# A hybrid attention step on one core: paced stores of k and v, loads given out when source and buffer are ready, and a second buffer

## The chip, the core and the metric

The kernel runs on one core of a Trainium2 chip. The core's engines each work through an instruction queue of their own: PE (TensorE) multiplies matrices, DVE (VectorE), ACT (ScalarE) and POOL (GpSimd) do the elementwise work, and SP issues most of the transfers between memory (DRAM) and the core. Engines wait for one another by semaphores. The metric is the device time of one execution in microseconds (us), lower is better.

## What is computed

One layer of a decoder in float32, for a prompt of 512 tokens and for 8 samples of 4 new tokens each with 1024 past tokens in paged caches. Both groups share the weights.

```python
def prompt_layer(x, norm_in, w_in, b_gate, b_forget, cmp_pe, cmp_w, w_out):
    h = rmsnorm(x, norm_in)
    q_n, kv_n, gates, z_n, q_f, k_f, v_f, logf, z_f = project(h, w_in, b_gate, b_forget)   # h @ w_in
    kc, c_end = compress(kv_n[:, :, 0], cmp_pe[0], cmp_w[0])      # blocks of 32 rows -> one row
    vc, _ = compress(kv_n[:, :, 1], cmp_pe[1], cmp_w[1])
    ...                                                           # per 128 queries:
    o_n = nsa_block(...)   # compressed + selected blocks + sliding window, gated
    o_f = fox_block(...)   # causal attention with a forget term
    y = merge(x, o_n, z_n, o_f, z_f, w_out)                       # silu gates, @ w_out, residual
    return y, (kv_n[:, :, :4], jnp.stack([k_f, v_f], axis=2), logf, kv_n[:, T - w_keep:, 4:])
```

The sample layer does the same with `cache_nsa_kv[page_table]`, `cache_fox_kv[page_table]` and `state_nsa_win` ahead of the new rows. A final RMSNorm follows. The new k and v rows are outputs too, in token order.

## The kernel before

The 544 tokens (512 of the prompt, 32 of the samples) stand in the columns of `h_hi` and `h_lo`, a two-part split of the normalized input. The main loop `run_tiles` computes the input projection in 60 tiles of 128 output columns. A tile is made of four weight pieces; a piece `raw` (128x512) is loaded by SP, split by ACT into `whi` and by DVE into `wlo`, and used by 24 matmuls into `pz` (three products for each of 4 row blocks and 2 token halves). Five `raw` buffers are loaded ahead, and pieces are split two ahead of their use. After a tile, `pz` is scaled into `zt` (two buffers), and the tile's `post` stream treats it: for k and v tiles `store_natural` transposes `zt` on DVE into `nat` (two buffers) and SP writes it to the output (`out<-nat`), to the scratch `scr_n` where a later stage reads it back, and its sample rows to `scr_s`.

All other work is written as Python generators, the streams: `fox_sample` (cache pages `fpg` with two buffers: score pages gathered by POOL and transposed by DVE into `ft`, value pages multiplied by PE into `accv`), `compress` (rows `crow`, tables `cw`, the prompt's own rows `cz` read back from `scr_n`, transposed by DVE into `more`; results go through `vt` to `scr_kc`), `nsa_prompt` (which loads a table of distances `rel_c` from `scr_c`), `nsa_sample` (pages `spg`, transposed into `skt`), the mixing, and the output projection `w_out` at the end.

The order of every engine's queue is set when the program is built. A planner, `Clock`, keeps a modelled time for each engine, for SP's ring (`ring`) and for each buffer. Between two groups of matmuls `S.pump()` runs every stream that may go on: a stream that says `yield [tile]` is resumed when the planner has the tile ready, `yield "flag"` when the flag is set, `yield function` when the function holds. On the chip, each engine takes its queue in exactly that order and waits at an instruction whose operands are not ready, with everything behind it. A load that is given out right after the last reader of its buffer stands in SP's or POOL's queue until that reader is done.

A flag such as `nkv00`, `k0` or `v0` releases the streams that read a stored tile, and `post{t}` allows tile t+2 to take its `zt` buffer. In the kernel before both are set after all of a tile's stores are given out, twelve or so in one go.

Pages are loaded half by SP and half by POOL. All instructions are recorded by one helper, so that every row of the profile says L147; the names of the tiles tell the places apart.

Of the kernel before, what the change touches and what calls it, by code (L numbers as in the profile page):

```python
# [8 lines left out]
F32 = mybir.dt.float32  # L9
# [6 lines left out]
P = 128  # L16
# [4 lines left out]
SEQ = 512  # L21
# [162 lines left out]
class Streams:  # L184
# [58 lines left out]

    def take_nat(self, n=1):
        yield lambda: self.left["nat"] >= n
        self.left["nat"] -= n
# [28 lines left out]
def trunk_step(ctx, tc, x_prompt, x_sample, cache_nsa_kv, cache_fox_kv, cache_fox_logf, state_nsa_win,  # L275
# [27 lines left out]
    flags = S.flags  # L303
# [110 lines left out]
    tiles = []  # L414
    raws, wsp, last_w, loaded = {}, {}, {}, [0]
# [69 lines left out]
    def run_tiles(t0, t1):  # L485
        for t in range(t0, t1):
# [6 lines left out]
            zt = stg.tile([P, TOK], F32, name="zt", bufs=2)  # L493
            clock.parts[zt.tensor.name] = (TOK, HALF)
# [201 lines left out]
    def store_natural(zt, dst_p, dst_s, keep_at=None):  # L696


        yield from S.take_nat()
        nat = stg.tile([P, TOK // 32, 32], F32, name="nat", bufs=2)  # L700
        yield [nat]
        nc.vector.transpose(nat.rearrange("p t f -> p (t f)"), zt)
        yield [nat]
        by_token = lambda ap, at, row, q: dram(ap, at + q * 32, [[row, 32], [32 * row, SEQ // 32], [1, 32]])
        for q in range(4):
            rows = nat[q * 32:q * 32 + 32]
            nc.sync.dma_start(by_token(*dst_p, q), rows[:, :SEQ // 32])
            if len(dst_s.ap) == 4:
                nc.sync.dma_start(dram(dst_s, q * 32, list(dst_s.ap)[1:]), rows[:, SEQ // 32])
            if keep_at is not None:  # L710
                nc.sync.dma_start(by_token(n_scr, keep_at * SEQ * P, P, q), rows[:, :SEQ // 32])
        if len(dst_s.ap) == 3:
            nc.sync.dma_start(dst_s, nat[:, SEQ // 32])
        if keep_at is not None and keep_at < 12:
            nc.sync.dma_start(dram(s_scr, keep_at * 32 * P, [[32, 4], [P, 32], [1, 32]]), nat[:, SEQ // 32])
        S.put_nat()
# [19 lines left out]
    def post_nkv(slot, kvh):  # L736
        def f(zt):
            if slot in (2, 4):
                nc.sync.dma_start(z_scr[28 + (slot - 2) + kvh], zt)
            yield from store_natural(zt, *dst_nsa(slot, kvh), {0: 12 + kvh, 1: 14 + kvh, 3: 8 + kvh, 5: 10 + kvh}.get(slot))  # L740
            flags.add(f"nkv{slot}{kvh}")
        return f
# [9 lines left out]
    def post_kf(h):  # L752
        def f(zt):
            nc.sync.dma_start(z_scr[16 + h], zt)
            nc.vector.tensor_copy(ks_f[:, h, :], zt[:, SEQ:TOK])
            yield from store_natural(zt, *dst_fox(h, 0))
            flags.add(f"k{h}")
        return f

    def post_vf(h):  # L760
        def f(zt):
            yield from store_natural(zt, *dst_fox(h, 1), h)
            flags.add(f"v{h}")
        return f
# [283 lines left out]
    def fox_sample(hh):  # L1048
# [48 lines left out]
        for kq in range(2):  # L1097
            acc = psum.tile([P, SEQ], F32, name="accv", tag="accv", bufs=1)
            for bq in range(2):
                for kp in range(2):  # L1100
                    ts = [fx.tile([P, 2, 1024], F32, name="ft", bufs=2) for _ in range(2)]
                    for x in range(2):
                        pg = pages[at[1]]
                        for half in range(2):
                            yield [pg, ts[half]]
                            nc.vector.transpose(ts[half][:, x].rearrange("p (a d) -> p a d", d=64),
                                                pg.rearrange("p a (g d) -> p (a g) d", g=4)[:, :, half * 64:half * 64 + 64])
                        at[1] += 1
                        ahead()
                    for half in range(2):  # L1110
                        yield [ts[half], acc]
                        scores(acc, half, bq, kp, ts[half])
            yield
            sl = s[:, kq * 512:(kq + 1) * 512]
            nc.vector.scalar_tensor_tensor(sl, acc, dcol, sl, op0=OP.add, op1=OP.add)
# [85 lines left out]
    def compress(pl):  # L1201
# [27 lines left out]
        for kv in range(2):  # L1229
            yield (f"nkv{kv}0", f"nkv{kv}1")  # L1230
            cz = pl.tile([P, 8, P], F32, name="cz")
# [24 lines left out]
        for step in steps + [None]:  # L1256
            if step:
# [11 lines left out]
                if bh == 0:  # L1269
                    cp(t[:, :, 256:], more[kv][:, cg * 4 + dp * 2:cg * 4 + dp * 2 + 2, :])  # L1270
                nc.vector.transpose(t[:, :, :256].rearrange("p c (a i) -> p a c i", i=32),
                                    gs[u].rearrange("p b (k v d) -> p b k v d", k=2, v=2)[:, :, kv, :, dp * 64:dp * 64 + 64])
                if kv and dp:
                    gs.pop(u)
                    load_rows(u + 2)
                yield
# [8 lines left out]
        for kv in range(2):  # L1285
# [4 lines left out]
            vt = pl.tile([P, 2, 8, 32], F32, name="vt")  # L1290
# [29 lines left out]
    def nsa_prompt(pl):  # L1320
# [9 lines left out]
        nc.vector.tensor_tensor(rel_p, rel_p, rm, op=OP.add)  # L1330
        nc.vector.tensor_scalar(rel_c, rel_c, jp[:, 0:1], None, op0=OP.add)
# [161 lines left out]
    def nsa_sample(pl):  # L1493
# [81 lines left out]
        for grp in range(2):  # L1575
# [78 lines left out]
            for br in range(2):  # L1654
# [16 lines left out]
                for half in range(nk // 256):  # L1671
                    kt = pl.tile([P, 2, 1024], F32, name="skt", bufs=2)
                    for x in range(2):
                        yield [got[0], kt]
                        nc.vector.transpose(kt[:, x], got.pop(0).rearrange("p a d -> p (a d)"))
# [67 lines left out]
            def set_values(k, **kw):  # L1743
                t = got.pop(0)
                values(k, [t[:, bb] for bb in range(4)], **kw)
                set_in()
            for k in range(8):
                yield [got[0]]
                set_values(k, first=k == 0)
# [3 lines left out]
            for k in range(8, 12):  # L1753
                yield [got[0]]
                set_values(k, last=k == 11)
# [318 lines left out]
```

## Time and profile before

| | |
|---|---|
| median of 3 runs | 1342.12 us (1339.14 to 1351.64) |
| profiled execution, its own time | 1346.01 us |
| its span in the profile | 1344.2 us |
| instructions in the span | 27395 |
| mean granted clock of PE | 0.983 |
| busy: PE / DVE / ACT / POOL | 1289.9 / 787.6 / 548.2 / 278.5 us |
| moved by DMA | 269.64 MB in 340658 packets |

Rows of a timeline read: start, duration, engine, line, operation, out<-in and shapes, count, and in brackets the idle time of the engine before it with what ended it. Rows of a window read: the window, its length, then busy time and count of PE, PE's weight loads, DVE, ACT and POOL, then PE's granted clock, the busy share of the DMA engines and GB/s. SPq is SP's issuing of a transfer; its duration is how long SP was held by it.

### The profile page before, as it was taken

Reading aid. Unit: us, or ns where it says so; the run is one execution under the profiler, and the core shown is the slowest. Engines: PE = TensorE matmul, PEld = TensorE weight load, DVE = VectorE, ACT = ScalarE, POOL = GpSimd, SP = SyncE. Lnnn points to the kernel's source line nnn. Section 1 sums busy time; section 2 is a strip of 40 time slices with the busy share of each in tenths; the row PEclk is TensorE's granted clock in tenths of the full one; section 3 lists DMA queues with packets and bytes.
Section 4 is the critical chain, followed back from the end, with each engine's and each line's share of the span. In section 5 each row is a group of like instructions: output and inputs, shape, how many; then the busy total and the mean of one; then the engine's idle time right before and its main releaser. Section 6 shows DMA issues by size and latency. Waiting matters only on the chain.

```text
span 1344.2 us, 27395 instructions
## 1 busy us (share of the span) xinstructions
PE 1289.9 (96%) x10133; PEld 1138.4 (85%) x10133; DVE 787.6 (59%) x1977; ACT 548.2 (41%) x1164; POOL 278.5 (21%) x357
## 2 busy tenths in 40 slices
PE   6989999999998999999999998979999999999997
PEld 4889998999998878999989897757788899777786
DVE  6735778876644446666787855442476545344256
ACT  5313333334432345766453541322357643333221
POOL 3310267633200120000365401213111000000000
PEclk8989999999998999999999999899999999999999
DMA  7576699987646987557578757999997873334423
GB/s 198 146 189 164 182 271 301 281 253 207 183 97 152 313 268 249 147 142 250 180 234 253 224 114 182 273 257 330 266 198 216 270 232 95 112 106 139 141 76 133
DMA packets 340658, 269.64 MB, mean 201 GB/s; under 512 B 118834, under 2 KB 288162, under 8 KB 339852
## 3 DMA queue, kind: packets, MB, share of 16 engines
q1 hardware_dynamic: 316364, 191.27, 51.6%
q0 software_dynamic: 24016, 76.10, 18.2%
q8 instruction: 79, 1.29, 0.4%
q14 instruction: 55, 0.45, 0.1%
q10 hardware_dynamic: 144, 0.52, 0.1%
HBM read 235.53 MB, written 40.61 MB: 205 GB/s over the span
## 4 chain that ended last, share of the span: by engine, by line
PE 74%; DMA 11%; SPq 4%; issue 3%; DVE 3%; POOL 3%; ACT 1%; POOLq 0%; DVEq 0%; ACTq 0%
PE pz L147 40%; PE po L147 15%; PE s L147 5%; PE accv L147 4%; PE tr L147 4%; SPq L147 4%; PE acc L147 3%; DMA spg<-in_cache_nsa_kv 2%; DMA fpg<-in_cache_fox_kv,fi 2%; POOL fpg L147 2%; DMA fpg<-in_cache_fox_kv 1%; PE psb L147 1%; PE accf L147 1%; DMA xt<-in_x_prompt 1%; DMA raw<-in_w_in 1%
## 5 line engine op out<-in xcount | busy, mean ns | idle before, releaser
L147 PE MATMUL pz<-h_hi,whi 128*128 128x272 f32 x1920 | 572.2, 298 | 2.3 <-ACT whi L147 2.3
L147 PE MATMUL pz<-h_hi,wlo 128*128 128x272 f32 x1920 | 557.9, 291 | 10.0 <-DVE wlo L147 9.9
L147 PE MATMUL pz<-h_lo,whi 128*128 128x272 f32 x1920 | 556.1, 290 | 0.0
L147 PEld LDWEIGHTS pz<-h_hi,whi 128*128 128x128 f32 x1920 | 365.4, 190 | 37.3 <-issue 31.9
L147 PEld LDWEIGHTS pz<-h_hi,wlo 128*128 128x128 f32 x1920 | 364.5, 190 | 11.1 <-DVE wlo L147 11.1
L147 PEld LDWEIGHTS pz<-h_lo,whi 128*128 128x128 f32 x1920 | 365.9, 191 | 0.6
L147 ACT ACTIVATE whi<-raw 128x512 fp32r<-128x512 f32 x275 | 171.4, 625 | 243.3 <-PE pz L147 130.2
L147 DVE TENSOR_TENSOR wlo<-raw,whi 128x512 fp32r<-128x512 f32 x275 | 186.1, 678 | 136.4 <-ACT whi L147 127.3
L147 POOL DMA_INDIRECT fpg<-in_cache_fox_kv,fi x128 | 128.9, 1007 | 223.3 <-ACT nptch L147 145.2
L147 POOL DMA_INDIRECT crow<-in_cache_nsa_kv,ci x64 | 65.3, 1020 | 156.1 <-DVE ct L147 125.2
L147 PE MATMUL po<-whi,h_hi 128*128 128x512 f32 (+1 forms) x256 | 95.6, 373 | 0.0
L147 PE MATMUL po<-wlo,h_hi 128*128 128x512 f32 (+1 forms) x256 | 93.9, 367 | 0.0
L147 PE MATMUL po<-whi,h_lo 128*128 128x512 f32 (+1 forms) x256 | 93.8, 367 | 0.0
L147 DVE TENSOR_TENSOR zt<-pz,rsb 128x272 f32<-128x272 f32 x67 | 29.6, 442 | 107.9 <-PE pz L147 107.9
L147 DVE STREAM_TRANSPOSE ft<-fpg 128x1024 f32<-128x1024 f32 x64 | 78.7, 1233 | 19.4 <-DMA fpg<-in_cache_fox_kv,fi 19.4
L147 POOL DMA_DIRECT2D fpg<-in_cache_fox_kv x64 | 35.3, 552 | 229.8 <-PE accv L147 179.5
L147 ACT ACTIVATE cxh<-ct 128x580 fp32r<-128x580 f32 (+1 forms) x64 | 42.3, 660 | 97.2 <-DVE ct L147 91.1
L147 PEld LDWEIGHTS po<-whi,h_hi 128*128 128x128 f32 x256 | 48.1, 188 | 20.2 <-ACT whi L147 7.5
L147 ACT ACTIVATE zt<-pz 128x272 f32<-128x272 f32 x54 | 21.5, 398 | 103.5 <-PE pz L147 103.3
L147 POOL DMA_DIRECT2D spg<-in_cache_nsa_kv x64 | 35.0, 547 | 131.8 <-DVE skt L147 51.4
L147 PEld LDWEIGHTS po<-whi,h_lo 128*128 128x128 f32 x256 | 48.1, 188 | 8.7
L147 PEld LDWEIGHTS po<-wlo,h_hi 128*128 128x128 f32 x256 | 48.2, 188 | 8.1
(409 smaller groups left out, 1931.4 us busy)
## 6 DMA issues: line engine op xcount, KB each, us to landing
raw<-in_w_in SPq DMA_DIRECT2D x240, 256.0 KB
fpg<-in_cache_fox_kv POOLq DMA_DIRECT2D x64, 256.0 KB, 6.1
fpg<-in_cache_fox_kv SPq DMA_DIRECT2D x64, 256.0 KB
raw<-in_w_out SPq DMA_DIRECT2D x40, 256.0 KB
spg<-in_cache_nsa_kv POOLq DMA_DIRECT2D x64, 128.0 KB, 6.4
spg<-in_cache_nsa_kv SPq DMA_DIRECT2D x64, 128.0 KB
spg<-in_state_nsa_win SPq DMA_DIRECT2D x64, 128.0 KB
out<-in_state_nsa_win SPq DMA_DIRECT2D x32, 254.0 KB
```

Source lines behind the costliest of these rows:

```text
L147: return fn(*a, **k)
```

## The change

The generators yield at more places, the stores of a tile are reordered and spread out, and one tile gets a second buffer. The mathematics and the matmuls stay as they are.

1. `S.quiet()` is a new condition: the planner's PE time is 1.0 us later than now, and SP's ring is at most 0.5 us ahead of PE.
2. `store_natural` sets `post{t}` as soon as `zt` is transposed. The stores that are read back (`scr_s`, then `scr_n` two by two with a `quiet` between) come first, then the flag is set; the outputs follow, one at a time with a `quiet` behind each.
3. In `fox_sample`, `nsa_sample` the next page is given out after `yield [page]`, when the planner has the last reader of the page done.
4. `compress` waits for `scr_n` before it gives out the loads of `cz`, and gives out the next rows (`load_rows`) after the next `yield`.
5. `vt` has two buffers.
6. `nsa_prompt` waits for `rel_c` before the first instruction on it.

```diff
+    def quiet(self):
+        until = self.clock.t["pe"] + 1.0
+        return lambda: self.clock.t["pe"] >= until and self.clock.ring <= self.clock.t["pe"] + 0.5
...
-    def store_natural(zt, dst_p, dst_s, keep_at=None):
+    def store_natural(zt, dst_p, dst_s, keep_at, flag):
         yield from S.take_nat()
         nat = stg.tile([P, TOK // 32, 32], F32, name="nat", bufs=2)
         yield [nat]
         nc.vector.transpose(nat.rearrange("p t f -> p (t f)"), zt)
+        flags.add(f"post{tile_of[zt.tensor.name]}")
         yield [nat]
...
+        rows = [nat[q * 32:q * 32 + 32] for q in range(4)]
+        if keep_at is not None:
+            if keep_at < 12:
+                nc.sync.dma_start(dram(s_scr, keep_at * 32 * P, [[32, 4], [P, 32], [1, 32]]), nat[:, SEQ // 32])
+            for q in range(4):
+                nc.sync.dma_start(by_token(n_scr, keep_at * SEQ * P, P, q), rows[q][:, :SEQ // 32])
+                if q % 2:
+                    yield S.quiet()
+        flags.add(flag)
+        yield ()
         for q in range(4):
-            rows = nat[q * 32:q * 32 + 32]
-            nc.sync.dma_start(by_token(*dst_p, q), rows[:, :SEQ // 32])
             if len(dst_s.ap) == 4:
-                nc.sync.dma_start(dram(dst_s, q * 32, list(dst_s.ap)[1:]), rows[:, SEQ // 32])
-            if keep_at is not None:
-                nc.sync.dma_start(by_token(n_scr, keep_at * SEQ * P, P, q), rows[:, :SEQ // 32])
+                nc.sync.dma_start(dram(dst_s, q * 32, list(dst_s.ap)[1:]), rows[q][:, SEQ // 32])
+            nc.sync.dma_start(by_token(*dst_p, q), rows[q][:, :SEQ // 32])
+            yield S.quiet()
         if len(dst_s.ap) == 3:
             nc.sync.dma_start(dst_s, nat[:, SEQ // 32])
-        if keep_at is not None and keep_at < 12:
-            nc.sync.dma_start(dram(s_scr, keep_at * 32 * P, [[32, 4], [P, 32], [1, 32]]), nat[:, SEQ // 32])
         S.put_nat()
...
# fox_sample, score pages
                         at[1] += 1
+                        yield [pg]
                         ahead()
...
# compress
             yield (f"nkv{kv}0", f"nkv{kv}1")
+            yield [dram(n_scr, (12 + kv * 2 + v) * SEQ * P, [[P, SEQ], [1, P]]) for v in range(2)]
             cz = pl.tile([P, 8, P], F32, name="cz")
...
+                yield
                 if kv and dp:
                     gs.pop(u)
                     load_rows(u + 2)
-                yield
...
-            vt = pl.tile([P, 2, 8, 32], F32, name="vt")
+            vt = pl.tile([P, 2, 8, 32], F32, name="vt", bufs=2)
...
# nsa_prompt
+        yield [rel_c]
         nc.vector.tensor_scalar(rel_c, rel_c, jp[:, 0:1], None, op0=OP.add)
...
# nsa_sample
                     for x in range(2):
-                        yield [got[0], kt]
-                        nc.vector.transpose(kt[:, x], got.pop(0).rearrange("p a d -> p (a d)"))
+                        t = got.pop(0)
+                        yield [t, kt]
+                        nc.vector.transpose(kt[:, x], t.rearrange("p a d -> p (a d)"))
+                        yield [t]
                         set_in()
...
             def set_values(k, **kw):
                 t = got.pop(0)
                 values(k, [t[:, bb] for bb in range(4)], **kw)
+                yield [t]
                 set_in()
```

Since the planner decides what comes next by its modelled times, these few lines move instructions on every engine. Three places are shown.

The first is SP's queue some 75 us into the run, where `cz`, the rows read back for `compress`, is loaded the first time. Before:

```order
L147 DMA out<-nat 32x16x32
L147 DMA scr_n<-nat 32x16x32
L147 DMA out<-nat 4x32x32
L147 DMA cz<-scr_n 16x8x128 x8
L147 DMA raw<-in_w_in 128x4x128
L147 DMA scr_f<-ft 4x32x128 x4
L147 DMA raw<-in_w_in 128x4x128 x4
```

And SP's queue at the same load in the changed kernel:

```order
L147 DMA out<-nat 4x32x32
L147 DMA scr_n<-nat 32x16x32 x2
L147 DMA raw<-in_w_in 128x4x128
L147 DMA scr_n<-nat 32x16x32 x2
L147 DMA scr_f<-ft 4x32x128 x4
L147 DMA out<-nat 32x16x32
L147 DMA cz<-scr_n 16x8x128 x8
L147 DMA raw<-in_w_in 128x4x128 x2
```

The four scratch stores of the tile stand ahead of its outputs, two by two around a weight piece, and one output instead of five stands between them and `cz`. On DVE the use of `cz` moved at the same place (`more` is what it is transposed into; the number is the buffer's):

```order
-L147 MEMSET more_982 128x32
-L147 COPY more_982<-peT 128x32
-L147 STREAM_TRANSPOSE more_982<-cz 128x32x32
-L147 TENSOR_TENSOR wlo<-raw,whi 128x512
-L147 TENSOR_TENSOR zt<-zt,rsb 128x272
+L147 TENSOR_TENSOR wlo<-raw,whi 128x512
+L147 TENSOR_TENSOR zt<-pz,rsb 128x272
+L147 STREAM_TRANSPOSE nat<-zt 128x544
+L147 TENSOR_TENSOR wlo<-raw,whi 128x512
+L147 MEMSET more_1063 128x32
+L147 COPY more_1063<-peT 128x32
+L147 STREAM_TRANSPOSE more_1063<-cz 128x32x32
```

Two weight pieces (`wlo`) are now split ahead of the transpose that waits for `cz`.

The second place is SP's queue in the second half, at the first value pages (`fpg`) of `fox_sample`; `fss` is the load of the sample rows just stored to `scr_s`, and an ISA row is the step that readies a page's address. Before:

```order
L147 DMA scr_n<-nat 32x16x32
L147 DMA out<-nat 32x16x32
L147 DMA scr_n<-nat 32x16x32
L147 DMA out<-nat 4x32x32
L147 DMA scr_s<-nat 4x32x32
L147 DMA fss<-scr_s 32x4x128
L147 ISA
L147 DMA fpg<-in_cache_fox_kv 128x512
```

And in the changed kernel:

```order
L147 DMA raw<-in_w_in 128x4x128 x3
L147 DMA scr_s<-nat 4x32x32
L147 DMA scr_n<-nat 32x16x32 x4
L147 DMA fss<-scr_s 32x4x128
L147 DMA out<-nat 32x16x32 x2
L147 ISA
L147 DMA fpg<-in_cache_fox_kv 128x512
L147 ISA
L147 DMA fpg<-in_cache_fox_kv 128x512
L147 DMA out<-nat 32x16x32
```

`scr_s` moved from the end of the tile's stores to their head, and two outputs instead of five stand ahead of the page.

The third place is PE's queue in the first half, at two neighbouring value pages (each `accv` row is one page; `pz` is the projection, `s` and `tr` belong to `nsa_prompt`). Before, with the next page only 32 rows behind the first:

```order
L147 MATMUL accv<-fpg,fpt 32x512 x4
L147 MATMUL s<-nkh,nqh 128x512
L147 MATMUL s<-nkl,nqh 128x512
L147 MATMUL s<-nkh,nql 128x512
L147 MATMUL tr<-ident,npc 16x128 x2
L147 MATMUL pz<-h_hi,whi 128x272
```

And in the changed kernel:

```order
L147 MATMUL accv<-fpg,fpt 32x512 x4
L147 MATMUL tr<-ident,npc 16x128 x2
L147 MATMUL pz<-h_hi,whi 128x272
L147 MATMUL pz<-h_lo,whi 128x272
L147 MATMUL pz<-h_hi,wlo 128x272
L147 MATMUL accv<-fpg,fpt 32x512 x4
```

The two pages stand five rows apart, and the pages after them follow correspondingly earlier.

More of the change, by code (lines that the diff above doesn't have):

```diff
@@ L414, in trunk_step @@
     tiles = []
+    tile_of = {}
     raws, wsp, last_w, loaded = {}, {}, {}, [0]
@@ L493, in run_tiles @@
             zt = stg.tile([P, TOK], F32, name="zt", bufs=2)
+            tile_of[zt.tensor.name] = t
             clock.parts[zt.tensor.name] = (TOK, HALF)
@@ L739, in f @@
                 nc.sync.dma_start(z_scr[28 + (slot - 2) + kvh], zt)
-            yield from store_natural(zt, *dst_nsa(slot, kvh), {0: 12 + kvh, 1: 14 + kvh, 3: 8 + kvh, 5: 10 + kvh}.get(slot))
-            flags.add(f"nkv{slot}{kvh}")
+            yield from store_natural(zt, *dst_nsa(slot, kvh), {0: 12 + kvh, 1: 14 + kvh, 3: 8 + kvh, 5: 10 + kvh}.get(slot), f"nkv{slot}{kvh}")
         return f
@@ L755, in f @@
             nc.vector.tensor_copy(ks_f[:, h, :], zt[:, SEQ:TOK])
-            yield from store_natural(zt, *dst_fox(h, 0))
-            flags.add(f"k{h}")
+            yield from store_natural(zt, *dst_fox(h, 0), None, f"k{h}")
         return f
@@ L761, in f @@
         def f(zt):
-            yield from store_natural(zt, *dst_fox(h, 1), h)
-            flags.add(f"v{h}")
+            yield from store_natural(zt, *dst_fox(h, 1), h, f"v{h}")
         return f
@@ L1748, in nsa_sample @@
                 yield [got[0]]
-                set_values(k, first=k == 0)
+                yield from set_values(k, first=k == 0)
             yield [vc]
@@ L1754, in nsa_sample @@
                 yield [got[0]]
-                set_values(k, last=k == 11)
+                yield from set_values(k, last=k == 11)
             yield
```

## The prediction

> **What bounds the kernel.** I read the busy shares of the page first, then the waits by engine, then the timeline of PE around each long wait, then the windows behind them for the granted clock.
>
> ```profile
> span 1344.2 us, 27395 instructions
> PE 1289.9 (96%) x10133; PEld 1138.4 (85%) x10133; DVE 787.6 (59%) x1977; ACT 548.2 (41%) x1164; POOL 278.5 (21%) x357
> ```
>
> PE is busy for 96% of the span, and the change takes no matmul out and adds none. What it can win is PE's idle time, some 54 us, and what the idle time does to PE's speed afterwards. The waits of PE say who causes it (us in total, times, longest):
>
> ```profile
> PE accv L147 <- DMA fpg<-in_cache_fox_kv: 11.9, 3, 6.8
> PE pz L147 <- DVE wlo L147: 9.9, 2, 6.0
> PE s L147 <- DVE skt L147: 2.4, 1, 2.4
> PE pz L147 <- ACT whi L147: 2.3, 1, 2.3
> ```
>
> Four groups hold 26.5 us in eight waits; the rest lies in the prologue, which the change does not touch, and in the tail after the last matmul. The single waits, in brackets, stand in PE's timeline:
>
> ```profile
> 87.60 0.59 PE L147 MATMUL pz<-h_hi,wlo 128*128 128x272 f32 x1 [5.95 <-DVE wlo L147]
> 399.88 0.59 PE L147 MATMUL pz<-h_hi,whi 128*128 128x272 f32 x1 [2.25 <-ACT whi L147]
> 418.80 0.59 PE L147 MATMUL pz<-h_hi,wlo 128*128 128x272 f32 x1 [3.94 <-DVE wlo L147]
> 841.28 2.79 PE L147 MATMUL accv<-fpg,fpt 128*32 128x512 f32 x8 [6.83 <-DMA fpg<-in_cache_fox_kv]
> 886.66 1.71 PE L147 MATMUL s<-skt,qb 128*32 128x256 f32 x27 [2.44 <-DVE skt L147]
> 906.96 2.63 PE L147 MATMUL accv<-fpg,fpt 128*32 128x512 f32 x8 [4.91 <-DMA fpg<-in_cache_fox_kv]
> ```
>
> Each of these costs more than its bracket. In the windows just behind them (the last three columns are granted clock, DMA share and GB/s; the second is PE's busy time) PE is busy but slow:
>
> ```profile
> 87.60:97.00 9.40, 9.40 (x56) 9.40 (x57) 3.00 (x5) 1.89 (x3) 0.00 (x0) 0.73 0.87 186
> 399.80:407.00 7.20, 7.12 (x43) 6.73 (x44) 3.71 (x7) 2.55 (x6) 0.00 (x0) 0.76 0.40 114
> 418.80:431.00 12.20, 12.20 (x80) 11.97 (x84) 7.45 (x15) 5.23 (x11) 0.00 (x0) 0.79 0.64 155
> 841.20:851.00 9.80, 9.71 (x52) 6.45 (x52) 2.03 (x5) 3.49 (x5) 1.12 (x2) 0.70 1.08 283
> 886.60:893.00 6.40, 6.34 (x62) 3.55 (x64) 3.26 (x12) 2.07 (x5) 1.07 (x2) 1.00 1.11 257
> 907.00:914.00 7.00, 7.00 (x41) 4.50 (x45) 0.88 (x1) 0.96 (x2) 2.20 (x5) 0.65 1.07 328
> 1086.00:1134.00 48.00, 48.00 (x385) 48.00 (x384) 21.92 (x45) 16.87 (x28) 0.00 (x0) 1.00 0.50 152
> ```
>
> The last row is PE undisturbed: 48.0 us at clock 1.00. Lost time is length times (1 - clock): 2.5 us behind 87.60, 1.7 behind 399.88, 2.6 behind 418.80, 2.9 behind 841.28, 2.5 behind 906.96, and none behind 886.66. So the six waits hold 26.3 us and 12.2 us of slow clock follow them: 38.5 us is the most there is to win.
>
> A rule of the Trainium skill, TensorE: Matmul & The Clock Gate, section "Part 1: The HAM clock gate", has the clock halved only after an idle window of about 3.4 us. By it the 2.25 us wait would leave no slow clock and the sum below would lose 1.7 us; the row behind 399.88 has 0.76, so the measurement decides for 1.7.
>
> **The change, term by term.** Durations are those of the profiled execution, whose own time is 1346.0 us, 3.9 above the median of 1342.1; the sum is made against 1346.0.
>
> *cz (two edits: stores first, loads after them).* What holds PE at 87.60 starts on SP:
>
> ```profile
> 75.67 0.57 SPq L147 DMA_DIRECT2D out<-nat  x1
> 76.29 7.30 SPq L147 DMA_DIRECT2D cz<-scr_n  x8
> 83.69 0.53 SPq L147 DMA_DIRECT2D raw<-in_w_in  x1
> 85.73 1.25 DVE L147 STREAM_TRANSPOSE more<-cz 128x1024 f32<-128x1024 f32 x1 [8.25 <-DMA cz<-scr_n]
> 86.84 0.63 ACT L147 ACTIVATE whi<-raw 128x512 fp32r<-128x512 f32 x1 [8.02 <-DMA raw<-in_w_in]
> ```
>
> The eight loads of cz keep SP for 7.3 us, the next weights wait behind them until 83.69, and DVE, which must make wlo, stands at the transpose of cz for 8.25 us. In the changed order the first transposes of cz stand two weight pieces later on DVE, and the scratch stores two by two ahead of the outputs. A weight piece feeds 24 matmuls of 125 ns (48.0 us for 384 in the last window), 3.0 us; counting the matmuls between the emission of the loads and the transposes, the lead grows from 8.7 to 13.0 us of PE's work for the first cz, and falls from 14.2 to 7.1 for the second. Issue and landing took 76.29 to 85.73, 9.4 us, behind a store burst. 13.0 covers it; 7.1 leaves up to 2.3 us, which the two weight pieces that are split ahead (6 us) cover. Bounds: all 5.95 stays if the loads are as slow as before and the cover is gone, or all goes with its slow clock. I take all: **-8.5 us**.
>
> *vt (second buffer).*
>
> ```profile
> 395.71 0.37 SPq L147 DMA_DIRECT2D scr_kc<-vt  x1
> 398.17 0.63 ACT L147 ACTIVATE vt<-s,bc 128x128 f32<-128x128 f32 x2 [7.40 <-DMA scr_kc<-vt]
> ```
>
> ACT waits 7.40 us to overwrite vt until its store has been read; whi queues behind it. With two buffers there is nothing to wait for; **-4.0 us** (2.25 and 1.7). What is late next is raw, issued early enough. Bounds: 0 to -4.0.
>
> *rel_c (one wait in the planner).*
>
> ```profile
> 413.26 0.35 SPq L147 DMA_DIRECT2D rel_c<-scr_c  x1
> 416.63 0.25 DVE L147 TENSOR_SCALAR rel_c<-rel_c,jp 128x64 f32<-128x64 f32 x1 [7.49 <-DMA rel_c<-scr_c]
> ```
>
> The small load took 3.4 us from issue, after standing behind a burst of natural stores. DVE now reaches it 4.3 us of PE's work after the load is emitted, with paced stores in between. It waits 1 us at worst, which the same 6 us cover: **-6.5 us** (3.94 and 2.6). Bounds: 0 to -6.5.
>
> *First value page of the second half.*
>
> ```profile
> 826.81 2.81 SPq L147 DMA_DIRECT2D out<-nat  x1
> 834.76 0.52 SPq L147 DMA_DIRECT2D scr_s<-nat  x1
> 837.34 0.94 SPq L147 DMA_DIRECT2D fpg<-in_cache_fox_kv  x2
> fpg<-in_cache_fox_kv POOLq DMA_DIRECT2D x64, 256.0 KB, 6.1
> ```
>
> The page's half on SP is issued at 837.34, behind a burst of natural stores of which the first row shows one that held SP for 2.81 us. In the changed order scr_s and four scr_n come first and two outputs only stand ahead of the page; but the page is needed 6.6 us of PE's work after its emission (11.3 before). From the issue to the matmul at 841.28 it took 3.9 us here; POOL's halves have a median of 6.1 from issue to landing (last row), and a store ahead like the one above adds up to 2.8. That makes 3.9 to 8.9 against 6.6. I take 3.0 of the 9.8 us (6.83 and 2.9) as staying: **-6.8 us**. Bounds: 0 to -9.8.
>
> *Later pages (the waits ahead of the next load, in scores and values).*
>
> ```profile
> 871.52 13.18 DMA spg<-in_cache_nsa_kv
> 885.64 5.87 DMA fpg<-in_cache_fox_kv
> 899.22 7.70 DMA fpg<-in_cache_fox_kv
> 820.00:910.00 90.00, 75.64 (x596) 55.17 (x595) 43.87 (x135) 24.22 (x40) 18.81 (x35) 0.92 0.99 255
> 910.00:980.00 70.00, 69.17 (x605) 54.77 (x605) 27.02 (x97) 22.96 (x46) 17.25 (x32) 0.99 1.00 281
> ```
>
> From the chain of waits and the windows: the transfers take 6 to 13 us because the DMA engines are full (0.99 and 1.00). The waits of 2.44 and 4.91 us with 2.5 of slow clock are 9.8 us. The changed order spreads the same pages over about 238 us of PE's work instead of 216, and 216 and 20 lost us were what they had; so the bytes fit without a wait, but only just. I take half: **-4.9 us**. Bounds: 0 to -9.8.
>
> *What it adds.* A load is now emitted when its buffer has been read, so that POOL and SP are not held by a load that cannot start; by itself that gives PE nothing. But in the first half value pages are consumed faster: from one page's last matmul to the use of the next page in that buffer stand 6.5 to 11.1 us of PE's work in the changed order (four of 14 pages under 7.1), 7.1 to 14.5 before.
>
> ```profile
> 440.00:520.00 80.00, 80.00 (x612) 63.03 (x611) 36.41 (x138) 36.34 (x89) 13.28 (x24) 1.00 0.91 293
> 502.60 0.88 SPq L147 DMA_DIRECT2D fpg<-in_cache_fox_kv  x2
> 509.97 1.06 PE L147 MATMUL accv<-fpg,fpt 128*32 128x512 f32 x8
> ```
>
> A page issued at 502.60 was there by 509.97, 7.4 us later, without a wait, so the shortest leads lose at most 0.9 us each: 3 us over the 14. The score pages, whose leads fall from 10-16 to 8-12 us, may lose 1.5. Together **+4.5 us**; 0 if pages land in 6.5 us, and 12 if a page takes 8.3 us (8.3 us of shortfalls, 2.5 of one slow clock, 1.5 for the gathers).
>
> Pacing (quiet) delays outputs alone; at 59% DVE and two nat buffers nothing on PE's path waits for them, and the tail is not touched: 0. If a nat buffer were held too long, the post of a tile would wait, not its zt, which is now given back right after the transpose.
>
> Sum: -8.5 - 4.0 - 6.5 - 6.8 - 4.9 + 4.5 = -26.2, so 1346.0 - 26.2 = 1319.8. The 3.9 us by which the median is lower I take to be part of the same waits, so I do not subtract them again: **1320 us**.
>
> **Rivals.**
> - *All goes.* The pages land in time everywhere and nothing new appears: 1346.0 - 38.5 = 1307. For it: the spread over 238 us. Against it: leads of 6.6 us.
> - *DMA stays the bound from 820 to 980.* The share of 0.99 speaks for it. Neither page term is won, the added one stays: -19.0 + 4.5, 1331.5.
> - *The stores still stand ahead.* Pacing is by the planner's clock, and all these loads stay on SP's queue; should it run late, cz, rel_c and the page are held as before and vt alone is won: 1342. In the Trainium skill, DMA: Bandwidth & Descriptors, section "Queues, rings and completion order", all that SP issues shares one row of rings whose descriptors are consumed in order; by that a load emitted behind an unfinished store waits for it whatever the flag says. The 7.3 us for eight cz loads agree.
> - *Slower: the value pages of the first half.* Two fpg buffers, leads of 6.5 to 11 us, DMA share 0.91. If a page took 11 us there, the fourteen shortfalls sum to 35 us and some four slow clocks of 2.5 follow: +45 in place of the +3, 1346.0 - 26.2 + 42 = 1362. It breaks even near 10 us a page. Against it: the 7.4 us above; for it, the 13.18 us of a page in the full stage.
>
> **How the numbers follow.** Forecast 0.52, all goes 0.12, DMA bound 0.19, stores ahead 0.10, slower 0.07. The range takes the bounds of all but the slower case: 1305 to 1343. One per cent, 13 us, is about what a measurement of this kernel can tell from no change: below 1329 lie the forecast (nearly all), "all goes" and a third of the DMA case, 0.67; within it 0.26; above 1355 the slower case, 0.07.
>
> **What would show it.** PE's waits for wlo, whi at 88, 400 and 419 gone, with clock 1.00 there; DVE's wait for cz under 2 us; ACT without a wait for vt; the 6.83 us wait under 4; value pages between 430 and 510 with new waits of about a microsecond. I am wrong if waits over 2 us appear at first-half value pages, if the DMA share near 0.99 brings new waits for spg and fpg, or if gathers of score pages hold DVE.

## The result and the profile after

| | kernel before | changed kernel |
|---|---|---|
| median of 22 runs, in turn | 1344.63 us (1339.14 to 1351.64) | 1335.23 us (1331.04 to 1346.97) |
| profiled execution, own time (span) | 1346.01 us (1344.2 us) | 1331.19 us (1329.5 us) |
| mean granted clock | 0.983 | 0.993 |

The ratio is 0.9938, with a 95% interval of 0.992 to 0.9955: 8 us less, where 22 to 26 were forecast. The same kernel gave 0.9897 (0.9875 to 0.992) and 0.9919 (0.9896 to 0.9941) in two later comparisons. The comparisons below ran on different chips; on one of them (e9 to e12) the kernel before took a median of 1413 us, so those numbers are read against that only.

PE's row of the page, to be laid beside that of before (1289.9 us busy of 1344.2):

```profile
PE 1286.2 (97%) x10133; PEld 1132.6 (85%) x10133; DVE 785.5 (59%) x1977; ACT 549.4 (41%) x1172; POOL 280.3 (21%) x357
```

PE's idle time fell from 54.3 to 43.3 us, its busy time by 3.7 us.

PE's waits in the changed kernel (us in total, times, longest), to be laid beside those of before:

```profile
PE accv L147 <- DMA fpg<-in_cache_fox_kv: 12.2, 3, 7.4
PE pz L147 <- DVE wlo L147: 4.4, 6, 1.7
```

The waits for wlo fell from 9.9 to 4.4 us, none over 1.75; whi and skt are gone from the list. The waits for value pages stayed: 11.9 us before, 12.2 after. PE's timeline shows where they stand now, in brackets:

```profile
109.92 0.39 PE L147 MATMUL pz<-h_hi,wlo 128*128 128x272 f32 x1 [1.51 <-DVE wlo L147]
226.15 0.39 PE L147 MATMUL pz<-h_hi,wlo 128*128 128x272 f32 x1 [1.75 <-DVE wlo L147]
845.15 2.76 PE L147 MATMUL accv<-fpg,fpt 128*32 128x512 f32 x8 [7.37 <-DMA fpg<-in_cache_fox_kv]
863.75 1.05 PE L147 MATMUL accv<-fpg,fpt 128*32 128x512 f32 x4 [2.55 <-DMA fpg<-in_cache_fox_kv]
867.10 1.92 PE L147 MATMUL accv<-fpg,fpt 128*32 128x512 f32 x4 [2.29 <-DMA fpg<-in_cache_fox_kv]
```

The windows that were slow before, and those behind the new waits (the last three columns are granted clock, DMA share and GB/s):

```profile
87.00:97.00 10.00, 9.95 (x79) 9.95 (x80) 4.71 (x8) 2.68 (x5) 0.00 (x0) 1.00 1.00 201
109.00:116.00 7.00, 6.08 (x48) 6.09 (x49) 6.49 (x12) 3.62 (x9) 0.00 (x0) 1.00 0.76 213
399.00:407.00 8.00, 8.00 (x66) 8.00 (x65) 2.61 (x7) 1.78 (x3) 0.00 (x0) 1.00 0.93 191
418.00:431.00 13.00, 13.00 (x102) 10.63 (x98) 6.87 (x31) 5.99 (x18) 3.23 (x6) 1.00 0.96 283
845.20:855.00 9.80, 9.80 (x78) 5.87 (x78) 4.28 (x6) 2.85 (x4) 1.07 (x2) 0.81 1.11 222
867.20:875.00 7.80, 7.80 (x38) 6.14 (x39) 0.00 (x0) 0.52 (x2) 1.07 (x2) 0.63 0.95 266
820.00:910.00 90.00, 77.79 (x662) 54.87 (x662) 31.38 (x63) 24.33 (x42) 23.91 (x45) 0.92 1.04 270
```

The three early places (the first, third and fourth row) have the full clock and no wait; the second row lies at the wait of 1.51 us. The stage from 820 to 910 us has hardly changed: PE is busy for 77.8 of 90 us (75.6 before) at clock 0.92, as before, and the DMA engines are as good as full (a share of 1.04, 0.99 before).

How the longest wait comes about stands on SP. Each half of the kernel has 16 value pages, and a page is four transfers, two by SP and two by POOL. The wait at 845 us is for the fifth page of the second half. Its buffer came free with the matmuls of the third page; POOL issued its half at 824.90, SP only at 836.42:

```profile
823.43 1.10 PE L147 MATMUL accv<-fpg,fpt 128*32 128x512 f32 x8
820.92 2.80 SPq L147 DMA_DIRECT2D out<-nat  x2
823.92 5.43 SPq L147 DMA_DIRECT2D spg<-in_cache_nsa_kv  x2
831.33 3.84 SPq L147 DMA_DIRECT2D spg<-in_cache_nsa_kv  x2
836.42 1.42 SPq L147 DMA_DIRECT2D fpg<-in_cache_fox_kv  x2
```

Two outputs and four loads of `spg` stood ahead of it on SP and held SP for 12 us in all. In the kernel before it was the third page whose half on SP came late (837.34), behind the burst of stores.

### The profile page after: what moved, and what is told of

Same layout as the page of the kernel before. It is cut to its first block, busy times and chain, and to the rows that moved or that the text cites. A ratio compares the mean times of both kernels' runs of the same rounds, so it can differ in the third digit from the quotient of the medians.

```text
span 1329.5 us, 27394 instructions
## 1 busy us (share of the span) xinstructions
PE 1286.2 (97%) x10133; PEld 1132.6 (85%) x10133; DVE 785.5 (59%) x1977; ACT 549.4 (41%) x1172; POOL 280.3 (21%) x357
## 4 chain that ended last, share of the span: by engine, by line
PE 74%; DMA 11%; DVE 5%; SPq 3%; issue 3%; POOL 2%; ACT 1%; DVEq 0%; ACTq 0%; POOLq 0%
PE pz L147 40%; PE po L147 15%; PE s L147 4%; PE tr L147 4%; PE accv L147 4%; PE acc L147 3%; SPq L147 3%; DMA spg<-in_cache_nsa_kv 2%; DMA spg<-in_state_nsa_win 2%; PE psb L147 1%; DMA raw<-in_w_in 1%; POOL fpg L147 1%; PE accf L147 1%; DMA fpg<-in_cache_fox_kv,fi 1%; DMA xt<-in_x_prompt 1%
## 5 line engine op out<-in xcount | busy, mean ns | idle before, releaser
L147 DVE TENSOR_TENSOR zt<-pz,rsb 128x272 f32<-128x272 f32 x57 | 25.1, 441 | 121.9 <-PE pz L147 121.9
L147 ACT ACTIVATE zt<-pz 128x272 f32<-128x272 f32 x64 | 25.4, 397 | 114.5 <-PE pz L147 113.2
```

Of the source, the lines that this page charges most:

```text
L147: return fn(*a, **k)
```

## The experiments

Each kernel is compared with the kernel before in turns of its own; "wait" is PE's idle time in front of a matmul, as in the rows above. A trace shows one execution, which can lie several us off the median of its kernel.

### One part of the change at a time (e1, e2, e3)

e1 has parts 4 to 6, e2 parts 1 and 2, e3 part 3 alone; of each one line:

```diff
e1  +            vt = pl.tile([P, 2, 8, 32], F32, name="vt", bufs=2)
e2  +                    yield S.quiet()
e3  +                        yield [pg]
```

> The kernel before with parts 4, 5 and 6 alone (the wait for scr_n before cz, load_rows behind the yield, two vt buffers, the wait for rel_c); stores and page loads as before. Theory A (the early waits are won one by one, each by its own part): ACT's wait of 7.4 us for vt and PE's 2.25 us are gone, the 3.9 us at rel_c is gone or under 1, together with their slow clocks about -10 us; cz, whose loads still stand behind the interleaved stores, keeps some 3 to 6 us. Ratio near 0.992. Theory B (a wait taken away early only moves to the next full stage, since the second half is bound by its transfers): ratio 0.996 to 1.000.

> The kernel before with parts 1 and 2 alone (stores that are read back first, the others paced, flags and zt earlier). Theory A: the wait behind cz at 88 us shrinks from 6 to 0-3 us and its slow clock goes, vt's 2.25 us stays, rel_c's 3.9 us shrinks to about 1: -8 us, ratio near 0.994. Theory B: the paced stores do nothing for PE, ratio 0.998 to 1.002.

> The kernel before with part 3 alone (the next page given out after the planner has the last reader done). Theory A (the stage from 820 to 910 us is bound by its transfers, whatever the order): waits for fpg and spg of 12 to 16 us in that stage as before, ratio 0.998 to 1.002. Theory C (part 3 makes pages late and so costs what the other parts win): more waits of PE for fpg, ratio 1.003 to 1.008.

Measured: e1 0.9966 (0.9948 to 0.9984), e2 1.0011 (0.9993 to 1.0028), e3 1.0019 (0.9993 to 1.0044). Each did its early work and lost it elsewhere. PE's rows of e1 and then e2:

```profile
91.52 0.39 PE L147 MATMUL pz<-h_hi,whi 128*128 128x272 f32 x1 [2.14 <-ACT whi L147]
642.32 0.65 PE L147 MATMUL accv<-ft,fqb 128*32 128x256 f32 x4 [5.86 <-issue]
```

```profile
398.64 0.40 PE L147 MATMUL pz<-h_hi,wlo 128*128 128x272 f32 x1 [2.04 <-DVE wlo L147]
637.99 0.61 PE L147 MATMUL accv<-ft,fqb 128*32 128x256 f32 x1 [3.98 <-issue]
873.27 1.74 PE L147 MATMUL accv<-fpg,fpt 128*32 128x512 f32 x4 [4.28 <-DMA fpg<-in_cache_fox_kv]
1011.30 1.11 PE L147 MATMUL tr<-ident,sp 128*128 128x128 f32 x4 [6.25 <-ACT sp L147]
```

In e1 the waits at 400 and 419 us are gone and that at 88 us is down to 2.1; in e2 those at 88 and 419 are gone and that at 399 stays, since vt has one buffer. So parts 4 to 6 and parts 1 and 2 do early what the prediction says of them. But in both a new wait stands near 640 us at the first score pages of the second half, and e2's longest, 6.25 us, is for ACT at 1011 us. Why these orders are late just there was not tested. (e1's trace is one of its slow executions, 1348 us against a median of 1341.) e3 still waits 4.5 us at 88 us and 1.7 at 410, as it should without the other parts. The three alone sum to -0.5 us (-4.6, +1.5, +2.6 by their ratios), all together to -8: the parts do not add. Theory A of e1 and e2 was wrong: e1 won less than half of what it said, e2 nothing, and both lie in the range of their theory B; the early microseconds that the rows show as won were given out again later. e3 has the ratio of its theory A.

### Taking one part out (e6, e7)

```diff
e6  -                        yield [pg]        (and the two  yield [t])
e7  -        return lambda: self.clock.t["pe"] >= until and self.clock.ring <= self.clock.t["pe"] + 0.5
e7  +        return lambda: True
```

> The changed kernel without part 3 (the next page is given out at once after the last reader again); all else changed. Theory A (part 3 is neutral, the stage is bound by transfers): ratio 0.991 to 0.996. Theory C (part 3 spreads the pages and makes some late): without it faster, 0.984 to 0.990. Theory D (part 3 gives the gathers of the first score pages of the second half their lead; the runs with parts 1 and 2 or 4 to 6 alone showed PE waiting 4.0 and 5.9 us there, at about 640 us): that wait comes back with a slow clock, ratio 0.996 to 1.002.

> The changed kernel with the pacing condition always true: stores in the new order, those read back first, but given out without pauses. Theory A (what counts early is the order, not the pauses): ratio 0.991 to 0.997. Rival (the pauses keep bursts of output stores out of the way of loads): waits of 2 us or more come back on PE behind cz, rel_c or the first value page, ratio 0.997 to 1.003.

Measured beside e8, the changed kernel itself (0.9897, 0.9875 to 0.992): e6 0.9923 (0.9907 to 0.9939), e7 0.9934 (0.9916 to 0.9953). Both intervals overlap with that of e8, so neither is told from it; by the medians (1335.9 and 1338.6 against 1333.4 us) part 3 and the pauses cost nothing and may be worth 3 to 5 us. By the ratios theory A holds for both. e7's rows show what the pauses do, on PE, SP and DVE:

```profile
84.98 0.57 PE L147 MATMUL pz<-h_hi,whi 128*128 128x272 f32 x1 [4.50 <-DVE zt L147]
73.60 7.62 SPq L147 DMA_DIRECT2D cz<-scr_n  x8
83.26 1.25 DVE L147 STREAM_TRANSPOSE more<-cz 128x1024 f32<-128x1024 f32 x1 [7.42 <-DMA out<-nat]
```

Without the pauses the eight loads of cz come right behind the stores again and hold SP for 7.6 us, DVE stands at the transpose for 7.4 (the row names an output as the last to land before it), and 4.5 of PE's 6 us are back. The rival holds at that place: the new order of the stores without the pauses does not carry it. Which effect of the pauses does this is not separated, since the planner moves other work with them: in the changed kernel the same loads still hold SP for 5.8 us and DVE still waits 4.3, but two weight pieces are split between, at 76.38 and 78.68 us; in e7 none is.

```profile
75.61 5.78 SPq L147 DMA_DIRECT2D cz<-scr_n  x8
83.78 1.25 DVE L147 STREAM_TRANSPOSE more<-cz 128x1024 f32<-128x1024 f32 x1 [4.32 <-DMA cz<-scr_n]
```

### The bytes of the full stage (e4, e5)

The pages of `nsa_sample` are loaded by half; the order and the number of transfers stay, each with half the rows. One of the edited lines:

```diff
-                    load_page(rows, cache_nsa_kv, ..., lambda c: c[0, :, 3].rearrange("p v d -> p (v d)"))
+                    load_page(rows, cache_nsa_kv, ..., lambda c: c[0, :, 3].rearrange("p v d -> p (v d)"), lambda a: a[:64])
```

> The changed kernel, with every selected-row and window page (spg) loaded by half: two of four row groups, or 64 of 128 rows, the same number of transfers and the same order on every engine; the transpose reads the loaded half twice and the products contract 64 rows instead of 128, so that half of the selected rows is left out. Theory A (transfers bound the stage): the bytes of the stage fall from about 15 MB by 2 MB, PE's waits of 7.4, 2.6 and 2.3 us for fpg and their slow clocks mostly go: 8 to 14 us less than the changed kernel, ratio to the kernel before 0.983 to 0.988. Rival (the page is issued too late, bytes do not matter): the 7.4 us wait stays above 5 us, ratio 0.992 to 0.995.

> The kernel before with the selected-row and window pages (spg) loaded by half in the same way as in the run with the changed kernel (half of the selected rows is left out, order and number of transfers unchanged). That run took 19 us off the changed kernel. Theory A (the full DMA engines hold the second half of both kernels, and the change wins only the early waits): before loses as much, 15 to 20 us, ratio 0.985 to 0.989, and the two halved kernels then differ by what the early waits and their slow clocks are worth, 7 to 13 us. Rival (the change moved the second half into a worse place, so that only the changed kernel is bound there): before loses under 8 us, ratio above 0.994.

Measured: e4 0.9798 (0.9774 to 0.9823), a median of 1316.35 us, more than its theory A said; e5 0.9903 (0.9887 to 0.9918), 1332.81 us. Against the full kernel the half takes 13 us off the kernel before (e5 lies between its two expectations), and off the changed one 0.010 to 0.014 of the ratio, by which of its three comparisons one takes, 13 to 19 us. The two halved kernels differ by 0.0105, 14 us. One window of e4 with SP's rows ahead of the fifth value page (L855 is the helper of this run), and the one long wait for a page that e5 keeps:

```profile
820.00:910.00 90.00, 88.74 (x791) 62.44 (x789) 33.62 (x77) 25.24 (x45) 25.49 (x48) 1.00 1.03 275
822.70 1.29 SPq L855 DMA_DIRECT2D spg<-in_cache_nsa_kv  x2
827.69 0.99 SPq L855 DMA_DIRECT2D spg<-in_cache_nsa_kv  x2
830.52 0.90 SPq L147 DMA_DIRECT2D fpg<-in_cache_fox_kv  x2
```

```profile
839.76 0.83 PE L147 MATMUL accv<-fpg,fpt 128*32 128x512 f32 x2 [4.36 <-DMA fpg<-in_cache_fox_kv]
```

In e4 PE is busy for 88.7 of the 90 us at full clock, with the DMA engines as full as before (1.03). The four `spg` loads ahead of the fifth page hold SP for 2.3 us instead of 9.3, the page's half on SP goes out at 830.52, and its matmuls at 836.29 do not wait. So at the longest wait the bytes (or the rows, which were halved with them) act by way of SP's queue. In e5 the third value page still waits 4.4 us (6.8 before): its half on SP is issued at 836.26, behind the burst of stores, which this run leaves in place, so the bytes of `spg` were at most a part of that wait. The waits of before at 887 and 907 us are gone; these, and the later ones of the changed kernel, go with the bytes of that stage. How much of the early gain the stage takes back, these two runs do not tell: 14 us between the halved kernels against 8 to 14 between the full ones.

### The changed kernel again (e8, f4)

> The changed kernel once more, for a second trace: its first profiled execution was 14.8 us under that of the kernel before, while the medians differ by 9 and its runs spread over 1331 to 1347 us. Theory A (what varies is when the pages of the full stage land): the waits up to 300 us and the first half's value pages repeat within 1 us, those between 820 and 990 us differ by several us. Rival (the early waits vary): waits of 2 us or more appear before 440 us in this trace.

> The changed kernel beside the three others of this comparison, third trace. All theories: ratio to before 0.989 to 0.995; waits for fpg of 5 us or more near 845 us and 2 us or more near 864 us.

The two traces had waits for value pages at 844 us (5.28) and 848 us (5.22), near 864 us (1.94 in e8, 1.32 in f4) and, in f4, at 870 us (3.18); SP issued its half of the fifth page at 836.91 and 840.11. The two early waits were 1.82 and 2.08 us in e8, 1.20 and 0.96 in f4. In e8 the early waits repeat within 0.4 us and the late ones shrink by 3 us in sum, as theory A says, though the 2.08 also just meets the rival's sign; f4 has its wait of 5 us, and of the 2 us expected near 864 only 1.32 there and 3.18 at 870. What repeats is the place, the size changes by some us.

### SP's queue or the DMA engines (e12, f3)

```diff
...
-                        load(rows, dram(state_nsa_win, at + 256, [[512, P], [1, 256]]))
+                        (nc.gpsimd if bb % 2 else nc.sync).dma_start(rows, dram(state_nsa_win, at + 256, [[512, P], [1, 256]]))
```

> The changed kernel with half of the window pages (every second sample's) issued by POOL instead of SP; bytes and buffers as before. It tells a full SP queue from full DMA engines: in the trace of the changed kernel the window pages hold SP for 2.1 to 4.9 us four times between 846 and 869 us, with pages of fpg behind them. Theory A (the DMA engines are full, whoever issues): PE's waits for fpg stay within 3 us in sum, ratio 0.990 to 0.995. Rival (SP's queue is what is full): the waits for fpg at 864 and 867 us go, 5 to 9 us, ratio 0.983 to 0.988.

> The changed kernel with half of the window pages issued by POOL instead of SP, again, beside the changed kernel itself. Theory A (the DMA engines are full, whoever issues): within 3 us of the changed kernel, PE's waits for fpg between 820 and 980 us 6 us or more in sum. Rival (SP's queue is what is full): 5 to 9 us under the changed kernel.

Measured: e12 0.9924 (0.9893 to 0.9955) where before took 1413 us, and f3 0.9906 (0.9881 to 0.9931) beside the changed kernel's 0.9919; theory A, by both ratios. In f3, whose trace is its slowest execution (1342.87 us against a median of 1332.39), the longest wait is still there:

```profile
852.74 1.07 PE L147 MATMUL accv<-fpg,fpt 128*32 128x512 f32 x2 [7.99 <-DMA fpg<-in_cache_fox_kv]
```

Who issues the window pages makes no difference that the times show. It does not follow that SP's queue is not what holds the pages. The window pages are issued from 846 us on in the changed kernel, after the fifth value page, so the edit cannot touch the longest wait: in f3 too SP is held by loads of the cached `spg` pages (4.46 and 2.86 us) and issues its half of the fifth page at 843.23. What the edit could touch are the waits at 864 and 867 us, 4.84 us in the changed kernel, 4.50 in f4 and 3.15 in f3. Whether the longest wait goes when the cached `spg` pages leave SP, or stand behind the value page, was not run.

### The planner's price of a transfer (e9, e10, e11, f1, f2, g1, g2)

The same bytes, with the planner's rate lowered, so that it expects a page later and puts more projection matmuls ahead of its use:

```diff
-            self.bus = max(self.bus, start + 0.65) + size / 320e3
+            self.bus = max(self.bus, start + 0.65) + size / 260e3
```

> The changed kernel with one number of the planner's model changed: its transfers move 300 instead of 320 KB a us, so that it gives loads out for a slower memory and orders the matmuls of the streams accordingly. Theory A (the stage from 820 us is bound by transfers that the planner counts as faster than the 231 to 280 GB/s they get): a more honest price puts more projection matmuls ahead of the pages, the waits for fpg shrink by a third: ratio 0.985 to 0.992. Rival (the order around the pages does not help, since the total of bytes in the stage stays): ratio 0.990 to 0.995, waits elsewhere.

> As the run with 300, with 280 KB a us. Theory A: the waits for fpg between 820 and 980 us shrink further, ratio 0.982 to 0.990. Rival: ratio 0.990 to 0.997.

> As the run with 300, with 260 KB a us, near what the stage gets. Theory A: few waits for fpg left, ratio 0.980 to 0.990. Rival: streams end later and something at the end (the mixing, the output projection) waits, ratio 0.990 to 1.005.

There (before at 1413 us) they gave 0.9978 (0.9946 to 1.001), 0.9817 (0.9766 to 0.9868) and 0.9699 (0.9655 to 0.9743), each outside the ranges it was expected in. In that comparison PE stood still in many short waits without a releaser, of which e9 has most; the changed kernel's list has none:

```profile
PE pz L147 <- issue: 28.9, 40, 1.8
```

The runs do not explain these, so 260 and 280 were run again beside the changed kernel:

> The changed kernel with the planner's price of transfers at 260 instead of 320 KB a us, again, since the runs of the planner's price were compared where the kernel before took 1413 us and PE stood still for 17 to 29 us more without a releaser. Theory A (the planner's too cheap transfers put the pages of the full stage too close): no PE wait over 3 us between 820 and 980 us, 4 to 12 us less than the changed kernel in the same comparison, ratio to before 0.982 to 0.988. Rival (the gain seen there came from those other stalls): equal to the changed kernel within 3 us, ratio 0.989 to 0.995.

> As the run with 260, with 280 KB a us. Theory A: between the changed kernel and the one with 260, ratio 0.984 to 0.991. Rival: 0.989 to 0.995.

Measured: f1 0.9773 (0.9747 to 0.9799), 1314.53 us; f2 0.9776 (0.9747 to 0.9804), 1315.93 us; the changed kernel beside them 1335.43 us. Some 20 us by one number, more than theory A of f1 said; f2 is not told from f1. f1 is the fastest full kernel of this study. Its rows of waits, window and pages (the fourth with the first and last start of the value matmuls, the last two SP's issues of `spg` and of its half of the fifth page):

```profile
PE accv L147 <- DMA fpg<-in_cache_fox_kv: 1.9, 2, 1.7
820.00:910.00 90.00, 87.38 (x784) 67.28 (x783) 36.51 (x74) 26.60 (x47) 21.65 (x40) 1.00 1.07 296
fpg<-in_cache_fox_kv POOLq DMA_DIRECT2D x24, 256.0 KB, 6.2
L147 PE MATMUL accv<-fpg,fpt x256: 592/593/617, 409.9 to 953.8; 128*32 128x512 f32 x128
812.39 1.07 PE L147 MATMUL accv<-fpg,fpt 128*32 128x512 f32 x8
825.57 1.02 SPq L147 DMA_DIRECT2D spg<-in_cache_nsa_kv  x2
826.91 0.90 SPq L147 DMA_DIRECT2D fpg<-in_cache_fox_kv  x2
```

The page rows and the first value matmuls of the second half in the changed kernel, and the row of the value matmuls before:

```profile
fpg<-in_cache_fox_kv POOLq DMA_DIRECT2D x28, 256.0 KB, 7.8
L147 PE MATMUL accv<-fpg,fpt x256: 592/593/1062, 415.2 to 931.9; 128*32 128x512 f32 x128
815.47 1.06 PE L147 MATMUL accv<-fpg,fpt 128*32 128x512 f32 x8
```

```profile
L147 PE MATMUL accv<-fpg,fpt x256: 592/605/1063, 430.8 to 942.5; 128*32 128x512 f32 x128
```

The value pages of the second half stand between 812 and 954 us in f1, 141 us, against 116 us (815 to 932) in the changed kernel and 121 us (822 to 943) before. From 815 to 930 us a page's half on POOL landed 6.2 us after issue in f1 and 7.8 in the changed kernel. Two loads of `spg` instead of four stand ahead of the fifth page on SP and hold it for 1.0 us, its half goes out at 826.91, and its matmuls at 839.29 do not wait. The DMA engines are as full (1.07), but move 296 GB/s instead of 270, and PE hardly stops. Full DMA engines alone, then, do not make PE wait, as e4 showed too. How the 20 us divide between the wider spacing, the order on SP and the other moves of the planner was not separated.

> The kernel before with the planner's price of transfers at 280 instead of 320 KB a us and nothing else; it is compared with the changed kernel at 280 (ratio 0.9776). Theory A (the price spreads the pages of the full stage, the change wins the early waits, and the two add up): the waits of 4.9 and 2.4 us near 900 us go, those at 88, 400 and 419 us may stay: ratio 0.988 to 0.994, 12 to 20 us above the changed kernel at 280. Rival (the price alone does it, also early): ratio 0.977 to 0.983.

> The changed kernel at 280 KB a us without part 3. Theory A (part 3 is neutral): 0.975 to 0.981. Rival (part 3 is what lets the planner spread the pages): the waits for fpg come back, 0.984 to 0.992.

Measured: g1 0.9949 (0.9931 to 0.9967), g2 0.9848 (0.9826 to 0.9871): g1 just above its theory A, g2 in the rival's range. PE's rows of g1, then of g2:

```profile
88.09 0.60 PE L147 MATMUL pz<-h_hi,wlo 128*128 128x272 f32 x1 [6.10 <-DVE wlo L147]
399.72 0.39 PE L147 MATMUL pz<-h_hi,whi 128*128 128x272 f32 x1 [2.92 <-ACT whi L147]
418.65 0.59 PE L147 MATMUL pz<-h_hi,wlo 128*128 128x272 f32 x1 [3.68 <-DVE wlo L147]
835.68 0.76 PE L147 MATMUL s<-kvc,qv 128*128 128x256 f32 x1 [6.29 <-DMA kvc<-scr_kc]
```

```profile
867.58 1.07 PE L147 MATMUL accv<-fpg,fpt 128*32 128x512 f32 x2 [4.47 <-DMA fpg<-in_cache_fox_kv]
```

With the price alone the kernel before keeps its early waits and wins 7 us; it also keeps a wait of 3.4 us for a value page, at 890 us, and the last row is a new one. At 280 the change is worth 0.9949 to 0.9776, some 23 us, close to the 26 of the forecast; and part 3, which seemed neutral at 320, is worth about 10 of them (0.9848 against 0.9776): without it a value page at 868 us waits 4.47 us. Both differences are between comparisons on two chips and good to some 5 us.

## Why the prediction was wrong

- **cz, vt, rel_c: the gain right, the reason in part.** The sum was -19.0 us. The three waits of PE and their slow clocks are gone, and ACT no longer waits for a store of vt. But DVE waits for cz 4.32 us at the first transpose (above) and 5.11 at the second, where under 2 were forecast, and 3.48 us for rel_c, where 1 was. The leads of 13.0 and 7.1 us were counted in the order of the program, and SP issues later than that: DVE stood at the first transpose 3.9 us after SP began to issue the loads, at the second 2.1 us after, and the loads took 8.2 and 7.2 us. What kept PE going is the second ground of the prediction, the weight pieces split ahead; it was all that was needed but for 1.5 us at 110 us, behind the second cz:

```profile
108.04 1.25 DVE L147 STREAM_TRANSPOSE more<-cz 128x1024 f32<-128x1024 f32 x1 [5.11 <-DMA cz<-scr_n]
381.98 0.26 DVE L147 TENSOR_SCALAR rel_c<-rel_c,jp 128x64 f32<-128x64 f32 x1 [3.48 <-DMA rel_c<-scr_c]
```

- **First value page: right, and more was won than taken.** The page so called is the third of the second half; the first two had been loaded long before. In the changed kernel it is used at 823.43, 6.8 us after SP issued its half, without a wait: all 9.8 us are gone, where 6.8 were taken.
- **Later pages: the step that failed.** The prediction took -4.9 because the changed order "spreads the same pages over about 238 us of PE's work instead of 216", so that the bytes fit without a wait. The runs show +7.1 in its place: waits of 7.37, 2.55 and 2.29 us with slow clocks of 1.9 (0.81 over 9.8 us) and 2.9 (0.63 over 7.8 us), 16.9 us, where 9.8 had been. The products of the spg pages did spread, from 192 us (868 to 1059) to 235 (827 to 1062); the value pages, for which PE waits, did not (121 us before, 116 after). And bytes over a whole stage do not say when one page goes out: the wait that the third page lost came back at the fifth, whose half on SP was issued 11.9 us after its buffer was free, behind stores and spg loads. With half the bytes (e4), or with fewer of these loads ahead of it (f1), that wait is gone. For the waits at 864 and 867 us SP's half of the page was issued at 854.69, 6.8 us after its buffer was free, and one transfer then took 11.2 us: there the transfer itself is slow.
- **What it adds: the size right by luck.** +4.5 was forecast, 3 of it at first-half value pages. There was no wait there; the 1.75 us at 226 us follow a wait of DVE for a gathered score page, and 1.5 us are cz's.
- **Sum.** -19.0 - 9.8 + 7.1 + 3.3 = -18.4; the profiled executions differ by 14.8 us. The waits in this sum take 10.9 us off PE's idle time, and it fell by 11.0. The slow clocks take 7.4 us off, but PE's busy time fell by 3.7 only; where the rest of it went the rows do not tell. The medians differ by 9.4 only: the profile of the changed kernel was one of its better executions, 4 us under its median, and that of before 1.4 over. What makes executions differ by several us stays open beyond the sizes of the page waits. (The four rows of waits in the prediction count seven waits, not eight; no sum uses the count.)
- **Rivals.** "DMA stays the bound from 820 to 980" came nearest, at 0.19: of the two page terms 2.7 us were won in sum. That its price of 1331.5 us is the profiled time (1331.19) is luck, since it leaves out those 2.7 us and the 3.7 us of busy time that did not go; it is 4 us under the median. It also named a full share as its ground, and e4 and f1 have that share without the waits. The slower rival had no sign: no first-half page was late. "The stores still stand ahead" did not happen at the page it named, and at cz not so that PE waits; e7 shows that it would there without pauses. The 7.3 us for eight cz loads, which this rival calls on, do not show loads waiting for stores: eight such loads hold SP for 5.2 to 6.0 us in the changed kernel's traces too, with one or two outputs right ahead of them.

The Trainium skill, TensorE: Matmul & The Clock Gate, section "Part 1: The HAM clock gate", states that the clock is halved after an idle window of about 3.4 us. As a threshold for one wait this does not hold here: before, 2.25 us at 400 us were followed by 0.76 over 7.2 us, and 2.44 us at 887 by 1.00; after, 1.51 us at 110 left 1.00, and 2.55 and 2.29 us within 3.4 us of one another left 0.63 over the next 7.8 us.

## What to carry to other kernels

Before counting a wait as won, follow the next pages on the queue that issues them: here the wait removed at the third page came back at the fifth, behind other loads on SP. A full DMA share is a warning and not a proof: e4 and f1 have it without the waits. When a planner decides the order, compare its rate with the rate of the full stage in the trace (320 KB a us against 255 to 270 GB/s here): correcting that one number gave some 20 us, about twice what the change did, and with it the change gave some 23, near what had been forecast for it. Test a change once more after the stage that hides it has been freed.

## What was not expected of the hardware

A full stage does not have a fixed rate: from 820 to 910 us, at a DMA share of 0.99 to 1.07, 255 GB/s were moved before, 270 after and 296 in f1, each with its own mix of pages. Nor has an issue a fixed price: of the 64 loads of cached `spg` pages that SP issues in the changed kernel, the median held it for 0.33 us, the longest for 3.86 (the second number and the third of the row).

```profile
L147 SPq DMA_DIRECT2D spg<-in_cache_nsa_kv x64: 316/333/3862, 791.2 to 1042.5; - x64
```

And the parts of a reordering do not add: three that measured -4.6, +1.5 and +2.6 us gave -8 to -14 together.
